# The last merged down step of each superblock: order of weight tile and token half, PSUM banks, and the columns of the last superblock

## The chip, the cores and the metric

The kernel runs on one core of a Trainium2 chip. A core has one matrix engine (TensorE, PE in the profile), three engines for elementwise work (VectorE or DVE, ScalarE or ACT, GpSimd or POOL), a queue engine that issues transfers (SyncE or SP) and 16 DMA engines. Matmul results land in PSUM, which has eight banks; all else lies in SBUF. The metric is the device time of one execution in microseconds. Before the change it is 2521.25 us, the median of 3 runs (2519.53 to 2521.3).

## The reference

One layer of a hybrid decoder runs over 2048 prompt tokens and 64 sample tokens of width 1024, all in fp32. Ahead of the MLP stand an RMS norm, one input projection, window attention and a pooling mixer side by side, an output projection, and cross attention into 256 memory tokens. What bears on the change is the MLP, the last norm, and the first lines of the next tokens:

```python
h = _rmsnorm(x, g_mix)
proj = h @ w_in
...
h = _rmsnorm(x, g_ffn)
x = x + jnp.square(jax.nn.relu(h @ w_up)) @ w_down
...
y_prompt = _rmsnorm(xp, g_final)
y_sample = _rmsnorm(xs, g_final)
```

`w_in` is 1024 x 1280, `w_up` 1024 x 4096 and `w_down` 4096 x 1024; the RMS norm is x * rsqrt(mean(x*x) + 1e-5) * g.

## The kernel before

**Tokens.** The 2112 tokens run in three superblocks of two blocks each, 384 + 384, then 256 + 320 (64 of them sample tokens), then 384 + 384. Activations are kept with the width of 1024 as eight pieces of 128 partitions (k or m from 0 to 7) and the tokens as columns. A superblock goes from the input projection (matmuls on L352 to L354) and attention through cross attention to the MLP, and is followed by the next one; the first superblock begins at once, the last one is followed by nothing.

**Numbers.** Each fp32 factor is split into a high and a low part, and each product takes three matmuls, high by high, high by low, low by high (`mm3`, L109 to L114). A weight tile of 128 x 1024 is fetched into one of six fp32 buffers f, and split by ACT (the high half, L118) and DVE (the low half, L119) into two of twelve buffers w.

**The MLP.** It runs over 16 pairs of 128-wide hidden tiles. For each, `up` makes the squared ReLU of both token halves in seven products, and `down` adds hidden times `w_down` to x. For the last two pairs there is one merged `down` with `fin=True`: 16 groups (8 output pieces m, 2 token halves h), each with 4 hidden tiles by 3 matmuls = 12 matmuls into one PSUM bank, after which DVE adds the bank to x (L1381). The weights come as two tiles, t = 0 for m from 0 to 3 and t = 1 for m from 4 to 7, each as four w buffers for two pairs. In the merged step the order is h outer, t inner: t=0 and t=1 for the first half, then both again for the second. All 16 groups take their bank from the four banks MM; the other four banks, AUX, serve norms and attention. In the second superblock the first half has the 256 columns of block 0 and 32 of block 1, the second half the other 288 of block 1; in the other two superblocks a half is a block.

**The last norm.** After each group of the merged step `Norm.sq` squares the finished piece on ACT and adds it to a running sum on DVE (L250). After the eighth piece of a block `final` takes the sum over partitions by one matmul with a matrix of ones (L258; in the last superblock's second block it is eight such matmuls, one for each piece, on L242), inverts the root with a logarithm, an exponential and three rows on DVE (L261 to L265), scales the eight pieces of x (L1402, eight rows) and sends them out in four transfers (L1404).

**What sets the order.** Weights are requested ahead in a fixed order by `Stream.pump`, up to five, as long as enough w and f buffers stay free. The next superblock's first weights (`in_win`) can therefore be requested only when the merged step gives back the w buffers of a tile. At that time the first block's x for the next superblock is fetched, normalised and split in pieces (`norm1_sums`, L300 to L302), the second block's from the hook at the fifth half-tile step on; each holds four of the six f buffers meanwhile. `flush` runs such deferred work a piece at a time, and `final` is deferred work as well (`DEFF` = 2 and 2: two flushes later). A scheduler then orders the rows of each engine; each engine executes its own rows in that order.

Of the kernel before, what the change touches and what calls it, by code (L numbers as in the profile page):

```python
# [14 lines left out]
P = 128  # L15
# [36 lines left out]
def kernel(ctx: ExitStack, tc: tile.TileContext, io, nW=12, nF=6, nT=10):  # L52
# [175 lines left out]
    class Norm:  # L228
        def __init__(self, n, x, on_pe=False, add=None):
            self.n, self.x, self.on_pe, self.add = n, x, on_pe, add or nc.vector  # L230
            self.acc = None
            self.pm = AUX.get() if on_pe else None

        def sq(self, k, eng=None):
            n = self.n
            if self.on_pe:
                t = TS.get()
                if eng is None:
                    nc.scalar.activation(t[:, 0:n], self.x(k), AF.Square)
                else:  # L240
                    eng.tensor_tensor(t[:, 0:n], self.x(k), self.x(k), ALU.mult)
                nc.tensor.matmul(self.pm[:, 0:n], ones[:], t[:, 0:n], start=k == 0, stop=k == 7)  # L242
# [4 lines left out]
            else:  # L247
# [3 lines left out]
                TS.put(t)  # L251

# [324 lines left out]
    def superblock(s, blks, nxt):  # L577
# [725 lines left out]
        def relu2(H, h, k, t):  # L1303
# [3 lines left out]
            hi, lo = H[4 * h + 2 * k], H[4 * h + 2 * k + 1]  # L1307
# [54 lines left out]
        def down(pl, Hs, fin=False, hook=None):  # L1362
            K = range(2 * len(pl))
            seq = [(t, h) for h in (0, 1) for t in (0, 1)] if fin else [(t, h) for t in (0, 1) for h in (1, 0)]
            loaded, left, steps = {}, {}, 0
            if fin:
                for bl in blks:
                    bl.norm = Norm(bl.n, bl.x, on_pe=last and bl.b == 1)
            for t, h in seq:
# [3 lines left out]
                w = loaded[t]  # L1373
                for m4 in range(4):
                    m = 4 * t + m4
                    ps = MM.get()
                    mm3(ps[:, 0:hn], K, lambda k: w8(w[k // 2][0])[:, 2 * m4 + k % 2, :], lambda k: w8(w[k // 2][1])[:, 2 * m4 + k % 2, :],
                        lambda k: Hs[k // 2][4 * h + 2 * (k % 2)], lambda k: Hs[k // 2][4 * h + 2 * (k % 2) + 1])
                    for bl, c0, o, n in halves[h]:
                        x = bl.x(m, c0, c0 + n)  # L1380
                        nc.vector.tensor_tensor(x, ps[:, o:o + n], x, ALU.add)  # L1381
                    if fin:
                        blks[h].norm.sq(m)
                    MM.put(ps)
                    if m4 == 3 or fin and m4 == 1:
# [9 lines left out]
                if fin and t == 1:  # L1395
                    later.append([DEFF[h], lambda h=h: final(blks[h])])

        def final(bl):
            bl.norm.fin()
            n = bl.n  # L1400
# [184 lines left out]
```

## Time and profile before

| what | value |
|---|---|
| time, median of 3 runs | 2521.25 us (2519.53 to 2521.3) |
| the profiled execution | 2526.65 us |
| its span in the trace | 2524.6 us |
| its mean granted clock of PE | 0.992 |
| busy: PE, DVE, ACT, POOL | 98%, 74%, 44%, 7% of the span |
| first matmul of the second superblock's input projection | 959.3 us |
| first matmul of the third one's | 1662.95 us |
| first matmul of the last merged step | 2472.86 us |

Times in the profile are microseconds from the span's start. A row of a timeline has start, length, engine, line, operation, output<-inputs and shape; `xN` at its end means N rows run together, and brackets give the idle time of the engine before it and what ended it. A row of a group has line, engine, operation, shapes and count, then the busy time, the mean ns of one, and the idle time ahead of it. Matmuls overlap their neighbours, so the distance between starts, not the length, is what one costs.

### The profile page before, as it was taken

The numbers are of one execution on the slowest core, as the hardware profiler recorded it, in microseconds if no ns is written. First come the engines' busy times: TensorE is split into PE (matmuls) and PEld (weight loads), VectorE is DVE, ScalarE is ACT, GpSimd is POOL, SyncE is SP. The second block draws the span as 40 slices with busy tenths as digits, with TensorE's granted clock in tenths as the row PEclk, the third lists the DMA queues.
The fourth block names the chain that finished last, engine by engine and source line by source line (L and its number), as shares of the span: only waits on it lengthen the run. The fifth ranks groups of instructions, "written<-read, shape, count | busy, mean of one in ns | idle before, by whom it ended". The sixth has DMA issues, their size and how long they took to land.

```text
span 2524.6 us, 38966 instructions
## 1 busy us (share of the span) xinstructions
PE 2479.4 (98%) x15199; PEld 2368.9 (94%) x15199; DVE 1860.2 (74%) x3687; ACT 1099.5 (44%) x2131; POOL 172.8 (7%) x282
## 2 busy tenths in 40 slices
PE   9999999999999999999999999989999999999998
PEld 8798989999999999896799999989998999999997
DVE  8668537877877787764698877888745877777775
ACT  7666335433333344653554434447534533333332
POOL 0015010000000001401000000003301000000000
PEclk9999999999999999899999999999999999999999
DMA  8833211122221125146633232240412122221211
GB/s 290 271 122 105 84 42 59 63 80 69 86 71 62 65 92 164 49 168 214 237 105 109 86 111 93 88 144 26 143 42 76 34 69 67 68 68 67 67 58 50
DMA packets 94844, 250.24 MB, mean 99 GB/s; under 512 B 17028, under 2 KB 31812, under 8 KB 93508
## 3 DMA queue, kind: packets, MB, share of 16 engines
q1 hardware_dynamic: 94660, 247.76, 29.5%
q8 instruction: 119, 1.95, 0.3%
q14 instruction: 65, 0.53, 0.1%
HBM read 225.03 MB, written 22.69 MB: 98 GB/s over the span
## 4 chain that ended last, share of the span: by engine, by line
PE 54%; DVE 3%; ACT 1%; DMA 1%; POOL 1%; issue 0%; POOLq 0%; DVEq 0%; ACTq 0%; SPq 0%
PE mm L112 8%; PE mm L113 8%; PE mm L114 7%; PE aux L114 5%; PE aux L113 5%; PE aux L112 5%; PE mm L354 4%; PE mm L353 4%; PE mm L352 4%; PE aux L772 1%; PE aux L803 1%; PE aux L1105 0%; DVE x L1402 0%; DVE w L119 0%; PE aux L1018 0%
## 5 line engine op out<-in xcount | busy, mean ns | idle before, releaser
L118 ACT CAST w<-f 128x1024 fp32r<-128x1024 f32 x378 | 395.7, 1050 | 723.3 <-PE mm L114 354.2
L119 DVE TENSOR_TENSOR w<-f,w 128x1024 fp32r<-128x1024 f32 x378 | 460.8, 1223 | 178.8 <-PE aux L113 93.3
L113 PE MATMUL mm<-act,w 128*128 128x384 f32 (+2 forms) x1812 | 578.6, 320 | 0.0
L114 PE MATMUL mm<-act,w 128*128 128x384 f32 (+2 forms) x1812 | 576.6, 319 | 1.9 <-DVE w L119 1.9
L112 PE MATMUL mm<-act,w 128*128 128x384 f32 (+2 forms) x1812 | 563.5, 321 | 3.6 <-ACT t L246 2.3
L352 PE MATMUL mm<-act,w 128*128 128x384 f32 (+2 forms) x1248 | 408.2, 327 | 5.6 <-DVE x L1381 4.0
L354 PE MATMUL mm<-act,w 128*128 128x384 f32 (+2 forms) x1248 | 404.5, 324 | 3.3 <-DVE w L119 3.1
L114 PE MATMUL aux<-act,w 128*128 128x384 f32 (+1 forms) x1260 | 404.1, 321 | 1.5 <-DVE w L119 1.5
L112 PE MATMUL aux<-act,w 128*128 128x384 f32 (+1 forms) x1260 | 405.2, 322 | 0.0
L113 PE MATMUL aux<-act,w 128*128 128x384 f32 (+1 forms) x1260 | 404.7, 321 | 0.0
L353 PE MATMUL mm<-act,w 128*128 128x384 f32 (+2 forms) x1248 | 404.3, 324 | 0.1
L1381 DVE TENSOR_TENSOR x<-mm,x 128x384 f32<-128x384 f32 (+3 forms) x672 | 314.3, 495 | 108.7 <-PE mm L114 104.5
L112 PEld LDWEIGHTS mm<-act,w 128*128 128x128 f32 x1812 | 337.6, 188 | 13.8 <-ACT act L1308 7.5
L113 PEld LDWEIGHTS mm<-act,w 128*128 128x128 f32 x1812 | 341.3, 188 | 5.1 <-DVE act L1309 3.7
L114 PEld LDWEIGHTS mm<-act,w 128*128 128x128 f32 x1812 | 340.9, 188 | 3.3 <-DVE w L119 2.3
L352 PEld LDWEIGHTS mm<-act,w 128*128 128x128 f32 x1248 | 238.1, 191 | 9.9 <-ACT w L118 2.7
L353 PEld LDWEIGHTS mm<-act,w 128*128 128x128 f32 x1248 | 238.1, 191 | 4.9 <-issue 2.3
L354 PEld LDWEIGHTS mm<-act,w 128*128 128x128 f32 x1248 | 238.1, 191 | 4.9 <-DVE w L119 4.5
L114 PEld LDWEIGHTS aux<-act,w 128*128 128x128 f32 x1260 | 237.0, 188 | 1.9 <-DVE w L119 1.8
L113 PEld LDWEIGHTS aux<-act,w 128*128 128x128 f32 x1260 | 237.0, 188 | 0.4
L112 PEld LDWEIGHTS aux<-act,w 128*128 128x128 f32 x1260 | 236.4, 188 | 0.4
L1323 DVE TENSOR_TENSOR t<-aux,t 128x384 f32<-128x384 f32 (+1 forms) x315 | 159.2, 519 | 21.6 <-PE aux L114 15.8
(229 smaller groups left out, 3022.0 us busy)
## 6 DMA issues: line engine op xcount, KB each, us to landing
f<-in_wup SPq DMA_DIRECT2D x96, 512.0 KB, 3.5
f<-in_wdn SPq DMA_DIRECT2D x96, 512.0 KB, 3.7
f<-in_win SPq DMA_DIRECT2D x30, 512.0 KB, 3.7
f<-a_s SPq DMA_DIRECT2D x24, 512.0 KB, 3.6
f<-b_s SPq DMA_DIRECT2D x24, 512.0 KB, 4.5
x<-in_x SPq DMA_DIRECT2D x6, 1536.0 KB, 7.4
f<-in_wco SPq DMA_DIRECT2D x16, 512.0 KB, 5.2
f<-in_cmk SPq DMA_DIRECT2D x16, 512.0 KB, 4.4
```

Source lines behind the costliest of these rows:

```text
L112: nc.tensor.matmul(ps, Wh(k), Hh(k), start=first and i == 0, stop=False)
L113: nc.tensor.matmul(ps, Wh(k), Hl(k), start=False, stop=False)
L114: nc.tensor.matmul(ps, Wl(k), Hh(k), start=False, stop=final and i == last)
L118: nc.scalar.copy(th[:], r[:, 0:1024])
L119: nc.vector.tensor_tensor(tl[:], r[:, 0:1024], f32(th[:]), ALU.subtract)
L352: nc.tensor.matmul(ps[:, 0:n], w8(th)[:, k, :], hi(b, k), start=k == 0, stop=False)
L353: nc.tensor.matmul(ps[:, 0:n], w8(th)[:, k, :], lo(b, k), start=False, stop=False)
L354: newest[0] = nc.tensor.matmul(ps[:, 0:n], w8(tl)[:, k, :], hi(b, k), start=False, stop=k == 7)
L772: nc.tensor.matmul(o, q[:, j, c0:c0 + P], kz[kv][hl][:, so + k0:so + 256], start=hl == 0, stop=hl == 1)
L803: nc.tensor.transpose(ps[:, P * j:P * j + P], u.Lv[:, j, P * kb:P * kb + P], ident[:])
L1323: nc.vector.tensor_tensor(t[:, 0:hn], ps[:, 0:hn], r[:, 0:hn], ALU.add)
L1381: nc.vector.tensor_tensor(x, ps[:, o:o + n], x, ALU.add)
```

## The change

It has four parts. In the first two superblocks the merged step runs the weight tile outside and the token half inside: t=0 for both halves, then t=1 for both. So the four w buffers of t=0 come free at half of the step, and a half's pieces are complete at three quarters (the first) and at the end (the second), where they were complete at a half and at the end. In all superblocks every second group takes its bank from AUX, so eight banks are in use. In the last superblock the halves still stand outside, but the columns are 512 (block 0 and 128 of block 1) and 256, where they were 384 and 384; the hidden tiles lie so that both halves are neighbours, and the deferred work advances after each group. There the last norm runs in three parts of 384, 128 and 256 columns, the last of them with seven squares added on DVE and two matmuls with ones in place of eight. The scaling is spread over flushes also in the last superblock, and y is written in strided transfers.

PE at the end of the second superblock's merged step, before. mm are the MM banks, aux the AUX banks, act the activations, w the weights; L114 is the merged step's last matmul, L352 to L354 are the next superblock's input projection. The ones matmul of block 0 stands 48 rows further ahead:

```order
L114 MATMUL mm0_109<-act13_76,w3_82 128x288
L352 MATMUL mm2_111<-act1_64,w1_80 128x384
L353 MATMUL mm2_111<-act4_67,w1_80 128x384
L352 MATMUL mm3_112<-act1_64,w8_87 128x384
L353 MATMUL mm3_112<-act4_67,w8_87 128x384
L352 MATMUL mm1_110<-act1_64,w0_79 128x384
L353 MATMUL mm1_110<-act4_67,w0_79 128x384
L352 MATMUL mm0_109<-act14_77,w1_80 128x384
L353 MATMUL mm0_109<-act6_69,w1_80 128x384
L354 MATMUL mm2_111<-act1_64,w9_88 128x384
```

The same place now (the lines 352 to 354 are 353 to 355 there):

```order
L114 MATMUL aux0_113<-act13_76,w3_82 128x288
L259 MATMUL aux1_114<-t0_97,ones_125 128x256
L353 MATMUL mm2_111<-act1_64,w1_80 128x384
L354 MATMUL mm2_111<-act4_67,w1_80 128x384
L355 MATMUL mm2_111<-act1_64,w9_88 128x384
```

The ones matmul of block 0 (L259) now stands directly behind the step and ahead of the projection, and the first projection group has its low half (L355) at once, not after four groups' high halves.

SP's requests in the same step, before: `in_x` is the second block's x, `in_win` the first weights of the next superblock.

```order
L543 DMA f2_93<-in_x 128x768
L543 DMA f4_95<-in_x 128x768
L543 DMA f1_92<-in_x 128x768
L543 DMA f3_94<-in_x 128x768
L137 DMA f0_91<-in_win 128x1024
L137 DMA f5_96<-in_win 128x1024
L137 DMA f2_93<-in_win 128x1024
L137 DMA f4_95<-in_win 128x1024
L1404 DMA out_y<-x0_107 128x512 x3
```

And now:

```order
L544 DMA f4_95<-in_x 128x768
L544 DMA f0_91<-in_x 128x768
L137 DMA f3_94<-in_win 128x1024
L137 DMA f5_96<-in_win 128x1024
L544 DMA f2_93<-in_x 128x768
L544 DMA f1_92<-in_x 128x768
L137 DMA f3_94<-in_win 128x1024
L137 DMA f5_96<-in_win 128x1024
L137 DMA f1_92<-in_win 128x1024
L137 DMA f4_95<-in_win 128x1024
L137 DMA f0_91<-in_win 128x1024
L1431 DMA out_y<-x0_107 128x512
```

Two weight requests moved ahead of the second half of the x requests, and the transfers of y from among the weights to behind them.

DVE at the end of the program, before: x is the block, t the norm's vectors, vec the gains.

```order
L1381 TENSOR_TENSOR x1_108<-mm0_109,x1_108 128x384
L263 SCALAR_TENSOR_TENSOR t8_105<-t5_102 128x384
L264 SCALAR_TENSOR_TENSOR t8_105<-aux3_116,t8_105 128x384
L265 SCALAR_TENSOR_TENSOR t5_102<-t8_105,t5_102 128x384
L1402 SCALAR_TENSOR_TENSOR x0_107<-x0_107,vec_129,t5_102 128x384 x8
L1381 TENSOR_TENSOR x1_108<-mm2_111,x1_108 128x384
L1381 TENSOR_TENSOR x1_108<-mm3_112,x1_108 128x384
L1381 TENSOR_TENSOR x1_108<-mm1_110,x1_108 128x384
L263 SCALAR_TENSOR_TENSOR t1_98<-t3_100 128x384
L264 SCALAR_TENSOR_TENSOR t1_98<-aux1_114,t1_98 128x384
L265 SCALAR_TENSOR_TENSOR t3_100<-t1_98,t3_100 128x384
L1402 SCALAR_TENSOR_TENSOR x1_108<-x1_108,vec_129,t3_100 128x384 x8
```

And now (L1406 is the addition to x, L1429 the scaling, L247 the sum of squares):

```order
L1406 TENSOR_TENSOR x1_108<-mm3_112,x1_108 128x256
L1429 SCALAR_TENSOR_TENSOR x1_108<-x1_108,vec_129,t2_99 128x128 x2
L247 TENSOR_TENSOR t8_105<-t8_105,t0_97 128x256
L1406 TENSOR_TENSOR x1_108<-aux1_114,x1_108 128x256
L1406 TENSOR_TENSOR x1_108<-mm1_110,x1_108 128x256
L1406 TENSOR_TENSOR x1_108<-aux2_115,x1_108 128x256
L247 TENSOR_TENSOR t8_105<-t8_105,t5_102 128x256
L247 TENSOR_TENSOR t8_105<-t8_105,t7_104 128x256
L264 SCALAR_TENSOR_TENSOR t3_100<-t6_103 128x256
L265 SCALAR_TENSOR_TENSOR t3_100<-aux3_116,t3_100 128x256
L266 SCALAR_TENSOR_TENSOR t6_103<-t3_100,t6_103 128x256
L1429 SCALAR_TENSOR_TENSOR x1_108<-x1_108,vec_129,t6_103 128x256 x8
```

The first part's scaling is no longer in one piece ahead of the last three additions, the last part has 256 columns instead of 384, and sums of squares are added on DVE.

The diff, cut to what matters:

```diff
@@ -229,17 +229,14 @@
         def __init__(self, n, x, on_pe=False, add=None):
             self.n, self.x, self.on_pe, self.add = n, x, on_pe, add or nc.vector
             self.acc = None
-            self.pm = AUX.get() if on_pe else None
-
-        def sq(self, k, eng=None):
+            self.pm = None
+
+        def sq(self, k):
             n = self.n
-            if self.on_pe:
+            if self.on_pe and k == 7:
                 t = TS.get()
-                if eng is None:
-                    nc.scalar.activation(t[:, 0:n], self.x(k), AF.Square)
-                else:
-                    eng.tensor_tensor(t[:, 0:n], self.x(k), self.x(k), ALU.mult)
-                nc.tensor.matmul(self.pm[:, 0:n], ones[:], t[:, 0:n], start=k == 0, stop=k == 7)
+                nc.scalar.activation(t[:, 0:n], self.x(k), AF.Square)
+                nc.tensor.matmul(self.pm[:, 0:n], ones[:], t[:, 0:n], start=False, stop=True)
                 TS.put(t)
             elif self.acc is None:
                 self.acc = TS.get()
@@ -249,6 +246,10 @@
                 nc.scalar.activation(t[:, 0:n], self.x(k), AF.Square)
                 self.add.tensor_tensor(self.acc[:, 0:n], self.acc[:, 0:n], t[:, 0:n], ALU.add)
                 TS.put(t)
+                if self.on_pe and k == 6:
+                    self.pm = AUX.get()
+                    nc.tensor.matmul(self.pm[:, 0:n], ones[:], self.acc[:, 0:n], start=True, stop=False)
+                    TS.put(self.acc)
 
         def fin(self):
             n = self.n
@@ -1304,7 +1305,7 @@
             for bl, c0, o, w in halves[h]:
                 nc.vector.scalar_tensor_tensor(t[:, o:o + w], t[:, o:o + w], 0.0, bl.r3[:, c0:c0 + w], ALU.max, ALU.mult)
             nc.scalar.activation(t[:, 0:hn], t[:, 0:hn], AF.Square)
-            hi, lo = H[4 * h + 2 * k], H[4 * h + 2 * k + 1]
+            hi, lo = H[4 * k + h], H[4 * k + 2 + h]
             nc.scalar.copy(hi, t[:, 0:hn])
             nc.vector.tensor_tensor(lo, t[:, 0:hn], f32(hi), ALU.subtract)
             TS.put(t)
@@ -1359,30 +1360,55 @@
             S.pump()
             return H
 
-        def down(pl, Hs, fin=False, hook=None):
+        def part(bl, c0, n):
+            p = FB()
+            p.bl, p.c0, p.n = bl, c0, n
+            p.x = lambda k: bl.x(k, c0, c0 + n)
+            return p
+
+
+        cols = []
+        for h in range(2):
+            cols.append((hn, (lambda h: lambda H, k, hl: H[4 * k + 2 * hl + h])(h), halves[h], [part(blks[h], 0, blks[h].n)]))
+        if last:
+            ends = []
+            b0, b1 = blks
+            for c0, n, pieces, parts in (
+                    (0, 512, [(b0, 0, 0, 384), (b1, 0, 384, 128)], [part(b0, 0, 384), part(b1, 0, 128)]),
+                    (512, 256, [(b1, 128, 0, 256)], [part(b1, 128, 256)])):
+                ends.append((n, (lambda c0, n: lambda W, k, hl: W[2 * k + hl][:, c0:c0 + n])(c0, n), pieces, parts))
+
+        def down(pl, Hs, fin=False, hook=None, cols=cols):
             K = range(2 * len(pl))
-            seq = [(t, h) for h in (0, 1) for t in (0, 1)] if fin else [(t, h) for t in (0, 1) for h in (1, 0)]
+            if fin and last:
+                seq = [(t, h) for h in (0, 1) for t in (0, 1)]
+            else:
+                seq = [(t, h) for t in (0, 1) for h in ((0, 1) if fin else (1, 0))]
             loaded, left, steps = {}, {}, 0
             if fin:
-                for bl in blks:
-                    bl.norm = Norm(bl.n, bl.x, on_pe=last and bl.b == 1)
+                for h in range(2):
+                    for p in cols[h][3]:
+                        p.norm = Norm(p.n, p.x, on_pe=last and h == 1)
             for t, h in seq:
                 if t not in loaded:
                     loaded[t] = [S.next(("dn", s, p, t)) for p in pl]
                     left[t] = 2
                 w = loaded[t]
+                n, mv, pieces, parts = cols[h]
                 for m4 in range(4):
                     m = 4 * t + m4
-                    ps = MM.get()
-                    mm3(ps[:, 0:hn], K, lambda k: w8(w[k // 2][0])[:, 2 * m4 + k % 2, :], lambda k: w8(w[k // 2][1])[:, 2 * m4 + k % 2, :],
-                        lambda k: Hs[k // 2][4 * h + 2 * (k % 2)], lambda k: Hs[k // 2][4 * h + 2 * (k % 2) + 1])
-                    for bl, c0, o, n in halves[h]:
-                        x = bl.x(m, c0, c0 + n)
-                        nc.vector.tensor_tensor(x, ps[:, o:o + n], x, ALU.add)
+                    bank = AUX if fin and m4 % 2 else MM
+                    ps = bank.get()
+                    mm3(ps[:, 0:n], K, lambda k: w8(w[k // 2][0])[:, 2 * m4 + k % 2, :], lambda k: w8(w[k // 2][1])[:, 2 * m4 + k % 2, :],
+                        lambda k: mv(Hs[k // 2], k % 2, 0), lambda k: mv(Hs[k // 2], k % 2, 1))
+                    for bl, c0, o, wd in pieces:
+                        x = bl.x(m, c0, c0 + wd)
+                        nc.vector.tensor_tensor(x, ps[:, o:o + wd], x, ALU.add)
                     if fin:
-                        blks[h].norm.sq(m)
-                    MM.put(ps)
-                    if m4 == 3 or fin and m4 == 1:
+                        for p in parts:
+                            p.norm.sq(m)
+                    bank.put(ps)
+                    if m4 == 3 or fin and (m4 == 1 or last):
                         steps += 1
                         if hook is not None:
                             hook(steps)
@@ -1393,18 +1419,19 @@
                         WS.put(*x)
                 S.pump()
                 if fin and t == 1:
-                    later.append([DEFF[h], lambda h=h: final(blks[h])])
-
-        def final(bl):
-            bl.norm.fin()
-            n = bl.n
+                    for i, p in enumerate(parts):
+                        later.append([(1 if last else DEFF[h]) + i, lambda p=p: final(p)])
+
+        def final(p):
+            p.norm.fin()
+            n, yo, bl = p.n, p.bl.xo + 8 * p.c0, p.bl
             for k in range(8):
-                nc.vector.scalar_tensor_tensor(bl.x(k), bl.x(k), vec[:, V_GFINAL + k:V_GFINAL + k + 1], bl.norm.r[:, 0:n], ALU.mult, ALU.mult)
+                nc.vector.scalar_tensor_tensor(p.x(k), p.x(k), vec[:, V_GFINAL + k:V_GFINAL + k + 1], p.norm.r[:, 0:n], ALU.mult, ALU.mult)
                 if k % 2 == 1:
-                    nc.sync.dma_start(io["y"][:, bl.xo + (k - 1) * n:bl.xo + (k + 1) * n], XT[bl.b][:, (k - 1) * n:(k + 1) * n])
-                    if has and k < 7:
+                    nc.sync.dma_start(io["y"][:, yo + (k - 1) * n:yo + (k + 1) * n].rearrange("p (k n) -> p k n", n=n), bl.xv[:, k - 1:k + 1, p.c0:p.c0 + n])
+                    if s > 0 and k < 7:
                         yield
-            TS.put(bl.norm.r)
+            TS.put(p.norm.r)
 
         S.resF = 0
         pre = roots(nxt or ())
@@ -1430,6 +1457,10 @@
             rest0 = norm1_sums(nxt[0])
         Hl = list(tt.values())
         H2 = up(NP - 1)
+        if last:
+
+            H, H2 = [[t[:, PT * i:PT * i + 2 * PT] for t in ts for i in (0, 2)] for ts in (Ht, [x for x in Hl if id(x) not in {id(y) for y in tt.values()}])]
+            cols = ends
         for bl in blks:
             TS.put(bl.r3)
         ACTS.put(*tt.values())
@@ -1439,7 +1470,7 @@
             S.resW = 4
             later.append([1, rest0])
             hook = lambda i: norm1(nxt[1], 1) if i == 5 else None
-        down([NP - 2, NP - 1], [H, H2], True, hook)
+        down([NP - 2, NP - 1], [H, H2], True, hook, cols)
         ACTS.put(*Ht, *Hl)
 
     TS2 = [sb(f"cp{i}", 512) for i in range(2)]
```

More of the change, by code (lines that the diff above doesn't have):

```diff
@@ L1567 @@
             n = npr + ns
-            yb = o["y"][:, 8 * xo:8 * (xo + n)].reshape(P, 8, n).transpose(2, 1, 0).reshape(n, 1024)
-            xo += n
+            ws = (128, 256) if t0 + npr == SEQ else (n,)
+            yb = []
+            for w in ws:
+                yb.append(o["y"][:, 8 * xo:8 * (xo + w)].reshape(P, 8, w).transpose(2, 1, 0).reshape(w, 1024))
+                xo += w
+            yb = np.concatenate(yb, 0)
             yp.append(yb[:npr])
```

## The prediction

> **What bounds the kernel now.** First the busy shares of the page, then the waits of TensorE (PE) at the end of the second superblock, then a table of stretches there.
>
> ```profile
> PE 2479.4 (98%) x15199; PEld 2368.9 (94%) x15199; DVE 1860.2 (74%) x3687; ACT 1099.5 (44%) x2131; POOL 172.8 (7%) x282
> PE mm L352 <- DVE x L1381: 4.0, 2, 2.4
> PE mm L354 <- DVE w L119: 2.4, 1, 2.4
> 1636.84:1662.95 26.11, 26.11 (x197) 25.82 (x195) 25.81 (x69) 17.65 (x40) 0.00 (x0) 1.00 0.37 108
> 1662.95:1671.82 8.87, 2.54 (x9) 1.36 (x9) 8.47 (x19) 4.52 (x9) 0.40 (x2) 0.81 0.38 135
> 1671.82:1675.70 3.88, 3.88 (x13) 3.88 (x14) 3.88 (x5) 0.00 (x0) 0.00 (x0) 0.56 0.89 287
> 1675.70:1720.00 44.30, 44.26 (x264) 43.15 (x263) 31.19 (x81) 20.27 (x49) 3.13 (x7) 1.00 0.27 96
> 1720.00:1800.00 80.00, 78.37 (x477) 72.92 (x477) 72.56 (x195) 61.89 (x162) 37.72 (x51) 1.00 0.25 86
> ```
>
> PE is busy 98% of the span, so the change can only win where PE stands still or runs cold: 45 us in all. (A windows row has time, length, busy time and count of PE, its weight loads, VectorE (DVE), ScalarE (ACT) and POOL, granted clock, DMA share, GB/s.) One such place is 1662.95 to 1675.70, directly behind the merged step of the second superblock. What those 22 matmuls would take at full speed comes from the start times of equal ones.
>
> ```profile
> 2485.09 0.33 PE L112 MATMUL mm<-act,w 128*128 128x384 f32 x1
> 2485.61 0.33 PE L112 MATMUL mm<-act,w 128*128 128x384 f32 x1
> 1890.23 0.39 PE L112 MATMUL mm<-w,act 128*128 128x512 f32 x1
> 1890.91 0.39 PE L112 MATMUL mm<-w,act 128*128 128x512 f32 x1
> 959.32 0.28 PE L352 MATMUL mm<-act,w 128*128 128x256 f32 x1
> 959.67 0.28 PE L352 MATMUL mm<-act,w 128*128 128x256 f32 x1
> ```
>
> Three matmuls lie between the two starts of a pair: 0.52/3 = 0.173 us for 384 columns, 0.68/3 = 0.227 for 512, 0.35/3 = 0.12 for 256. So 22 x 0.173 = 3.8 us of work took 8.87 + 3.88 = 12.75: **9.0 us are lost**. DVE was busy in 25.81 of the 26.11 us before and 8.47 of the 8.87 in it: PE waits for DVE.
>
> **The boundary after the second superblock.** What DVE does there, grouped by form from 1641.7 to 1672, with the first and last DVE rows and the first weight request:
>
> ```profile
> L300 DVE SCALAR_TENSOR_TENSOR t<-f,vec,t 128x384 f32<-128x384 f32 x13 | 7.6, 611 | 0.0
> L302 DVE TENSOR_TENSOR act<-t,act 128x384 fp32r<-128x384 f32 x14 | 7.5, 551 | 0.4 <-ACT act L301 0.4
> L1381 DVE TENSOR_TENSOR x<-mm,x 128x288 f32<-128x288 f32 x8 | 3.4, 449 | 0.0
> L250 DVE TENSOR_TENSOR t<-t,t 128x320 f32<-128x320 f32 x7 | 3.4, 486 | 0.1
> L1402 DVE SCALAR_TENSOR_TENSOR x<-x,vec,t 128x256 f32<-128x256 f32 x6 | 2.7, 479 | 0.0
> L263 DVE SCALAR_TENSOR_TENSOR t<-t 128x256 f32<-128x256 f32 x1 | 0.4, 419 | 0.0
> L119 DVE TENSOR_TENSOR w<-f,w 128x1024 fp32r<-128x1024 f32 x1 | 1.2, 1221 | 0.0
> 1641.70 1.28 DVE L1381 TENSOR_TENSOR x<-mm,x 128x256 f32<-128x256 f32 x5
> 1670.55 1.22 DVE L119 TENSOR_TENSOR w<-f,w 128x1024 fp32r<-128x1024 f32 x1
> 1649.44 11.98 SPq L137 DMA_DIRECT2D f<-in_win  x4
> 1659.12 0.30 ACT L97 CAST w<-kcar 64x128 fp32r<-64x128 f32 x1
> ```
>
> Before, the first weight split's low half (L119) is DVE's last row, at 1671.77, and PE's first L354 starts just then, at 1671.82. In the new order the weight tile of t=0 is free at half of the step instead of three quarters, so its requests and split stand earlier; and the second half's pieces, the final norm of block 0 and its scaling stand later. PE's first row behind the step is now the ones matmul of block 0 (L259), which waits for the last add of block 0's squares on DVE. I counted which DVE rows stood ahead of L119 and now stand behind that add: 5 of L300, 6 of L302, 4 evictions of 288 columns, 4 adds of 320, the 3 Newton rows (L263 to L265) and 6 of L1402; one more L119 stands ahead of it. Rows that follow each other overlap by about 0.08 us, so each costs its mean less that: 5 x 0.53 + 6 x 0.47 + 4 x 0.37 + 4 x 0.40 + 3 x 0.34 + 6 x 0.40 - 1.14 = 10.8. The 30.07 us from 1641.70 to 1671.77 shrink to 19.2, that is to 1660.97.
>
> To this I add an estimated 2 to 2.6 us, since block 0's last squares run on ACT behind the cast of the carry (L97), which in its turn waits for the matmul group that reads the buffers it overwrites, and now stands ahead of those squares. That row began at 1659.12; its price is bounded by nothing and by the 4.52 us that ACT worked in 1662.95 to 1671.82. So the sum is ready at 1663 to 1663.6; PE comes there at about 1662.4, as one fp32 ones matmul of some 0.5 us no longer stands before it. PE waits about 1.3 us including the releases, then about 0.6 and 0.7 for the third and the later weights, whose L119 come one by one at 1.14. Of 9.0 about 2.6 stay and some of the cooled clock: **6 us gained**, with ends 0 and 9. The two waits for the eviction (4.0 in the waits view) go by the eight banks; alone they would only become waits for L119, since the split comes last.
>
> On SP the four y stores of a block now stand behind the weight requests instead of among them, and the second block's x requests between those; DMA was 0.37 and 0.38 busy there, so I cost the queue at nothing.
>
> What is moved behind this point (some 12 us of DVE) costs nothing where DVE has slack: 44.30 - 31.19 = 13.1 us from 1675.70 to 1720. After 1720 DVE is at 72.56 of 80 us, so what is still owed there would come out of PE; I take 0, with 2 as upper bound (inside the end of 0 gained).
>
> **The boundary after the first superblock.** Same move, but nothing to win:
>
> ```profile
> 956.00:984.00 28.00, 28.00 (x199) 27.54 (x198) 27.46 (x56) 11.38 (x22) 7.08 (x8) 1.00 0.66 207
> 984.00:1000.00 16.00, 16.00 (x127) 15.77 (x126) 8.63 (x30) 3.76 (x10) 0.00 (x0) 1.00 0.41 117
> 956.14 4.32 DVE L1402 SCALAR_TENSOR_TENSOR x<-x,vec,t 128x384 f32<-128x384 f32 x8
> ```
>
> PE never waits there. DVE is full until 984 (27.46 of 28), and the eight L1402 of a block, 4.32 us in one piece here, now stand between the evictions of the in-projection. With eight banks in flight and 16.00 - 8.63 = 7.4 us of slack behind I take 0; a block of 4.32 in front of a bank that PE wants is the upper price, and below nothing there is no gain, as PE has no idle time to give.
>
> **The tail.** In the last superblock the order stays, the columns become 512 + 256, and the norm sums of the second part are added on DVE.
>
> ```profile
> 2506.41 4.32 DVE L1402 SCALAR_TENSOR_TENSOR x<-x,vec,t 128x384 f32<-128x384 f32 x8
> 2510.65 1.48 DVE L1381 TENSOR_TENSOR x<-mm,x 128x384 f32<-128x384 f32 x3
> 2515.22 0.56 DVE L263 SCALAR_TENSOR_TENSOR t<-t 128x384 f32<-128x384 f32 x1 [3.09 <-ACT t L262]
> 2517.00 4.32 DVE L1402 SCALAR_TENSOR_TENSOR x<-x,vec,t 128x384 f32<-128x384 f32 x8
> 2510.72 0.34 PE L114 MATMUL mm<-act,w 128*128 128x384 f32 x1
> 2511.81 2.20 PE L242 MATMUL aux<-t,ones 128*128 128x384 f32 x6 [0.75 <-ACT t L239]
> 2507.59 14.10 SPq L1404 DMA_DIRECT2D out_y<-x  x8
> ```
>
> The columns by themselves give nothing: 0.227 + 0.12 against 2 x 0.173. Before, three evictions stand behind the eight L1402 of block 0 and end at 2512.1; three ones matmuls (2.20, two rows each, so 0.735 for one), logarithm and exponential (1.2, from 2514.01 to 2515.22) and three Newton rows (1.78, to 2517.00) follow, then eight L1402 to 2521.32, and 3.3 us for the last store to 2524.6. After: the step begins at 2472.86 as before; its 192 matmuls take 96 x 0.227 + 96 x 0.12 = 33.3, with about 1.2 for the ones matmuls of the first part PE ends at 2507.4. DVE is the later one in the second part, 2494.9 on: eight evictions and six adds of 256 (14 x 0.34 = 4.8), 16 scalings (8 x 0.53, and 8 x 0.25 for 128 columns, estimated from 0.53 for 384 and 0.40 for 256: 6.2), Newton rows of 384 and 128 (2.5), what is left of the first part (1.5), 15.0 in all, and some 1.2 of waits: the last eviction ends near 2511.1, the last add at 2511.8. Then, scaled down from the rows for 384, two ones matmuls of 256 (0.5 each) to 2512.9, logarithm and exponential 0.9, Newton 1.35, eight scalings at 0.40 to 2518.4, and 3.3 for the store: 2521.7 against 2524.6, 2.9 gained. PE is idle for 4.4 us ahead of the last ones matmuls and may be cold for them, 1 us more. **2 us gained**, with ends 1 and 4.
>
> How long an idle time cools PE is shown once more here, by a small hole and what follows:
>
> ```profile
> 1000.00:1004.00 4.00, 3.60 (x28) 3.00 (x27) 1.22 (x4) 3.79 (x14) 1.21 (x3) 1.00 0.00 0
> 1004.00:1008.00 4.00, 3.00 (x17) 2.43 (x16) 2.78 (x7) 1.75 (x6) 1.46 (x2) 0.77 0.20 49
> 1008.00:1020.00 12.00, 12.00 (x51) 11.04 (x52) 1.95 (x7) 1.37 (x5) 0.00 (x0) 0.50 0.35 120
> 1880.00:1920.00 40.00, 40.00 (x191) 33.11 (x189) 16.93 (x32) 16.52 (x39) 6.57 (x14) 1.00 0.16 54
> ```
>
> 1.4 us of idle in 8 us is followed by 12 us at half clock. So even the short waits that I leave at 1663 may cost some clock, which is why I take 6 and not 6.4.
>
> The Trainium skill ("TensorE: Matmul & The Clock Gate", section "HAM oscillation — how this bites in real kernels") has the rule that only idle gaps above some 3.4 us cost clock. By it the waits left at 1663 would cost nothing beyond themselves (6.4 in place of 6), and the tail's 4.4 us would cool PE; the row of 0.50 speaks against it for the first.
>
> **Rivals.** *The waits go altogether*: ACT's cast isn't late and the low halves come in time; 9 + 3, 2509. For it speaks that 10.8 us of DVE work leave the path; against it that PE's first row is a wait for DVE. *The wait is replaced*: DVE stays full as before, and the moved rows come back between the first splits, so at most 2 at the boundary and 2 in the tail: 2517.3 to 2519. For it speaks that DVE worked 25.81 of 26.11 us before, against it the 13.1 us of slack behind. *Slower*: at the first boundary the L1402 of each block hold back an eviction whose bank PE needs next: 4.3 us of wait, and half clock behind it as in 1671.82 to 1675.70, where 13 x 0.173 = 2.25 took 3.88, 1.6 more; two blocks 11.8. With nothing won at the second boundary and 2 in the tail this gives 2531. It needs the bank to be asked for within the 4.3 us; it is slower as soon as both blocks do that and less than 10 are won elsewhere. *512 columns run cold*: half clock in the 96 matmuls of 512 columns, 96 x 0.227 = 21.8 more, 2535. Against it stand such matmuls at 1.00 in the stretch from 1880 to 1920, PE busy 40.00 of 40.
>
> The Trainium skill (the same page, "A second HAM failure mode: psum-queue depth-cycling") tells of a kernel that cycled PSUM banks at 512 columns and swung between half and full clock; that is this last rival, and the trace of 1880 to 1920 disagrees.
>
> **How the numbers follow.** The profiled execution took 2526.65 us (span 2524.6), 5.4 above the median of 2521.25; I subtract the same 8 from both: 2518.65 for such an execution, **2513.3** for the median. Chances: forecast (2510 to 2516) 0.50, waits gone 0.18, wait replaced 0.25, slower 0.05, cold columns 0.02. 0.2%, about what a measurement of this kernel can tell from no change, is 5 us: faster is below 2516.2 (0.50 + 0.18 = 0.68), same up to 2526.3 (0.25), slower 0.07. The range takes in the second rival down to 2508 and most of the third up to 2518.5; outside are the two slow cases and the edges, some 0.15.
>
> **What would show it.** Right: behind the second merged step PE's waits sum to 2 to 3 us in place of 7.5, the first of them an L259 waiting for a DVE add, and the clock stays above 0.9 by 1675; no PE idle time between 950 and 1000; the last L1429 ends some 2.9 us sooner against the step's first matmul. Wrong: L259 or L355 waits over 4 us, DVE full until 1690, L98 evictions waiting at 960 to 980 behind L1429, a clock below 1 in the 512-column part, or PE, not DVE, late in the tail.

## The result, and the profile after

The changed kernel takes 2509.73 us (median of 5 runs, 2507.94 to 2512.65) against 2521.3 us before (median of 5, 2519.53 to 2525.3): ratio 0.995, 95% interval 0.9938 to 0.9961, so 9.8 to 15.6 us less. Forecast were 2513.3 us and a gain of 8. In later series of the kernel before, the medians were 2524.18 us (35 runs) and 2523.97 (11 runs), so the 11.6 us between the two medians here are rather low than high. The profiled execution took 2509.73 us, its span 2507.9.

The page, PE's waits behind the second merged step (window 1600 to 1720), and stretches of the changed kernel, to be held against those of before:

```profile
PE 2467.2 (98%) x15189; PEld 2354.5 (94%) x15189; DVE 1865.3 (74%) x3719; ACT 1101.3 (44%) x2141; POOL 168.9 (7%) x282
PE mm L355 <- DVE w L119: 0.7, 1, 0.7
PE mm L353 <- DVE w L589: 0.2, 1, 0.2
PE aux L773 <- DVE st L774: 0.2, 1, 0.2
```

```profile
1600.00:1654.87 54.87, 54.87 (x415) 54.75 (x414) 46.72 (x106) 29.00 (x56) 0.00 (x0) 1.00 0.36 112
1654.87:1675.00 20.13, 19.76 (x111) 18.91 (x110) 19.87 (x44) 10.06 (x20) 0.55 (x2) 1.00 0.48 157
1675.00:1720.00 45.00, 44.04 (x268) 41.58 (x268) 38.09 (x111) 28.34 (x77) 6.04 (x13) 1.00 0.23 80
1720.00:1800.00 80.00, 79.20 (x473) 74.27 (x472) 63.09 (x159) 52.03 (x130) 36.74 (x48) 1.00 0.32 106
```

Where 12.75 us held 22 matmuls, the 20.13 us from 1654.87 hold 111 rows of them at a clock of 1.00. Of waits 1.1 us are left, where the view of before has 4.0 + 2.4 = 6.4 (the 7.5 that the prediction and the expectation for the order alone name for them stand in no view). DVE is still full (19.87 of 20.13), but with work that nobody waits for; the moved rows show from 1675 to 1720, where DVE is at 38.09 of 45.00 instead of 31.19 of 44.30, and PE is not hurt.

To see where the rest went, the start of the same matmul was read in both traces; between two rows of the table the difference changes only by what lies between them.

| place | before | after | difference |
|---|---|---|---|
| end of the first superblock's MLP | 904.24 | 903.03 | -1.2 |
| in-projection of the second | 989.46 | 988.14 | -1.3 |
| behind its attention | 1109.60 | 1104.45 | -5.2 |
| start of its MLP | 1289.89 | 1284.73 | -5.2 |
| end of its MLP | 1620.57 | 1612.99 | -7.6 |
| in the third superblock | 1807.74 | 1792.67 | -15.1 |
| ahead of the last merged step | 2470.09 | 2455.01 | -15.1 |
| end of the span | 2524.6 | 2507.9 | -16.7 |

So 7.5 us come from the boundary behind the second superblock and 1.6 from the tail. But 2.4 come from inside the second superblock's MLP, where no order changed, and 3.9 from 989 to 1110, where nothing was forecast. 1.2 lie ahead of the first merged step, where only the place of the hidden slices differs; two executions of the kernel before differ by 2.75 us at the same matmul, so nothing can be read from these 1.2. The profiled execution before was 5.4 us above its median, so these terms (16.7) are more than the medians' 11.6.

### The profile page after: what moved, and what is told of

It is laid out like the page before. It is cut to its first block, busy times and chain, and to the rows that moved or that the text cites. A ratio compares the mean times of both kernels' runs of the same rounds, so it can differ in the third digit from the quotient of the medians.

```text
span 2507.9 us, 38993 instructions
## 1 busy us (share of the span) xinstructions
PE 2467.2 (98%) x15189; PEld 2354.5 (94%) x15189; DVE 1865.3 (74%) x3719; ACT 1101.3 (44%) x2141; POOL 168.9 (7%) x282
## 4 chain that ended last, share of the span: by engine, by line
PE 53%; DVE 4%; ACT 1%; DMA 1%; POOL 1%; issue 1%; POOLq 0%; SPq 0%; DVEq 0%; ACTq 0%
PE mm L112 7%; PE mm L113 7%; PE mm L114 7%; PE aux L114 6%; PE aux L112 6%; PE aux L113 6%; PE mm L355 4%; PE mm L354 4%; PE mm L353 4%; PE aux L773 1%; DVE x L1429 1%; DVE w L119 1%; PE aux L804 1%; DMA f<-in_cmk 0%; POOL t L691 0%
## 5 line engine op out<-in xcount | busy, mean ns | idle before, releaser
L119 DVE TENSOR_TENSOR w<-f,w 128x1024 fp32r<-128x1024 f32 x378 | 461.2, 1224 | 176.8 <-PE aux L113 93.4
L113 PE MATMUL mm<-act,w 128*128 128x384 f32 (+2 forms) x1716 | 546.7, 319 | 0.0
L114 PE MATMUL mm<-act,w 128*128 128x384 f32 (+2 forms) x1716 | 544.7, 318 | 1.8 <-DVE w L119 1.8
L112 PE MATMUL mm<-act,w 128*128 128x384 f32 (+2 forms) x1716 | 533.5, 320 | 4.3 <-DVE t L460 2.2
L114 PE MATMUL aux<-act,w 128*128 128x384 f32 (+2 forms) x1356 | 435.0, 321 | 1.5 <-DVE w L119 1.5
L112 PE MATMUL aux<-act,w 128*128 128x384 f32 (+2 forms) x1356 | 436.0, 322 | 0.0
L113 PE MATMUL aux<-act,w 128*128 128x384 f32 (+2 forms) x1356 | 435.9, 321 | 0.0
L353 PE MATMUL mm<-act,w 128*128 128x384 f32 (+2 forms) x1248 | 406.9, 326 | 2.1 <-ACT act L728 1.8
L355 PE MATMUL mm<-act,w 128*128 128x384 f32 (+2 forms) x1248 | 402.6, 323 | 2.3 <-DVE w L119 2.1
L354 PE MATMUL mm<-act,w 128*128 128x384 f32 (+2 forms) x1248 | 402.3, 322 | 0.9 <-DVE act L729 0.9
L1406 DVE TENSOR_TENSOR x<-mm,x 128x384 f32<-128x384 f32 (+3 forms) x648 | 302.3, 494 | 93.9 <-PE mm L114 90.3
L112 PEld LDWEIGHTS mm<-act,w 128*128 128x128 f32 x1716 | 320.0, 189 | 14.5 <-ACT act L1309 7.6
L113 PEld LDWEIGHTS mm<-act,w 128*128 128x128 f32 x1716 | 323.6, 189 | 5.7 <-DVE act L1310 3.5
L114 PEld LDWEIGHTS mm<-act,w 128*128 128x128 f32 x1716 | 323.7, 189 | 3.1 <-DVE w L119 2.2
L114 PEld LDWEIGHTS aux<-act,w 128*128 128x128 f32 x1356 | 255.0, 188 | 2.6 <-DVE w L119 1.8
L113 PEld LDWEIGHTS aux<-act,w 128*128 128x128 f32 x1356 | 255.1, 188 | 1.1
L112 PEld LDWEIGHTS aux<-act,w 128*128 128x128 f32 x1356 | 254.5, 188 | 0.9
L353 PEld LDWEIGHTS mm<-act,w 128*128 128x128 f32 x1248 | 236.4, 189 | 6.8 <-ACT act L728 2.4
L354 PEld LDWEIGHTS mm<-act,w 128*128 128x128 f32 x1248 | 236.5, 189 | 6.3 <-issue 2.3
L355 PEld LDWEIGHTS mm<-act,w 128*128 128x128 f32 x1248 | 236.3, 189 | 4.1 <-DVE w L119 3.8
```

The costliest lines, as they stand in the source:

```text
L112: nc.tensor.matmul(ps, Wh(k), Hh(k), start=first and i == 0, stop=False)
L113: nc.tensor.matmul(ps, Wh(k), Hl(k), start=False, stop=False)
L114: nc.tensor.matmul(ps, Wl(k), Hh(k), start=False, stop=final and i == last)
L119: nc.vector.tensor_tensor(tl[:], r[:, 0:1024], f32(th[:]), ALU.subtract)
L353: nc.tensor.matmul(ps[:, 0:n], w8(th)[:, k, :], hi(b, k), start=k == 0, stop=False)
L354: nc.tensor.matmul(ps[:, 0:n], w8(th)[:, k, :], lo(b, k), start=False, stop=False)
```

## The experiments

**One part at a time.** Four kernels, each the kernel before with one part of the change. The order alone:

```diff
-            seq = [(t, h) for h in (0, 1) for t in (0, 1)] if fin else [(t, h) for t in (0, 1) for h in (1, 0)]
+            if fin and last:
+                seq = [(t, h) for h in (0, 1) for t in (0, 1)]
+            else:
+                seq = [(t, h) for t in (0, 1) for h in ((0, 1) if fin else (1, 0))]
```

> The kernel before with one part of the change: the weight tile outside, the token half inside, in the merged steps of the first two superblocks. Theory A (PE at 1662.95 waits for the DVE queue, and the order takes 10.8 us of DVE work from ahead of the first split): most of the boundary's gain comes from this alone, 5 to 8 us, and PE's waits there fall from 7.5 to under 3 us. Rival B (PE waits for PSUM banks, as the waits view names L1381 for 4.0 of them): the order alone gives at most 3 us, and PE still waits 4 us for evictions.

Measured: ratio 0.9976 (0.9966 to 0.9986), 6.0 us. PE's waits from 1640 to 1720 of this kernel:

```profile
PE mm L354 <- DVE w L119: 0.9, 1, 0.9
PE mm L112 <- DVE x L1384: 0.7, 2, 0.4
PE mm L352 <- DVE x L1384: 0.5, 1, 0.5
```

2.1 us are left of 6.4; in its trace the same matmuls gain 5.4 us between 1624 and 1807 of before. That is the boundary's part; the 6.0 us of the ratio are of the whole program. Theory A holds, with 1.2 us of eviction waits (L1384 is the addition to x here) left.

The eight banks alone:

```diff
-                    ps = MM.get()
+                    bank = AUX if fin and m4 % 2 else MM
+                    ps = bank.get()
...
-                    MM.put(ps)
+                    bank.put(ps)
```

> The kernel before with eight PSUM banks in the three merged steps and nothing else. Theory A: within 1 us of before; the two waits for L1381 at 1662.95 turn into waits for the weight split L119 with the same sum, 7 to 8 us, since the split stays last on DVE. Rival B: 4 us faster, the waits for L1381 go and nothing takes their place.

Measured: ratio 0.9991 (0.998 to 1.0001). PE's waits from 1600 to 1720:

```profile
PE mm L354 <- DVE w L119: 5.0, 1, 5.0
PE mm L352 <- DVE x L1382: 1.9, 1, 1.9
```

6.9 us of waits in place of 6.4 and as much time lost as before: its matmuls stand 3.1 us ahead at 1624 and 3.0 at 1807. Most of the wait moved by name from the eviction to the split, as A said (5.0 for L119; one eviction, L1382, is still waited for, 1.9): the name of a wait is not its price. The 2.3 us of the ratio aren't resolved from nothing.

The place of the hidden slices alone:

```diff
-            hi, lo = H[4 * h + 2 * k], H[4 * h + 2 * k + 1]
+            hi, lo = H[4 * k + h], H[4 * k + 2 + h]
...
-                        lambda k: Hs[k // 2][4 * h + 2 * (k % 2)], lambda k: Hs[k // 2][4 * h + 2 * (k % 2) + 1])
+                        lambda k: Hs[k // 2][4 * (k % 2) + h], lambda k: Hs[k // 2][4 * (k % 2) + 2 + h])
```

> The kernel before with only the places of the hidden tiles' slices changed as in the change (high and low part two slices apart in one tile, not neighbours). Theory A: the 288-column matmuls of the second superblock's down steps run at 0.132 us instead of 0.1345, 12 of them 0.03 us sooner, 2 to 2.5 us over the superblock, and nothing in the other superblocks with 384 columns. Rival C: that drift of 2.4 us between the two traces belongs to the execution, not to the program: 0 us, pitch 0.1345 as before.

Measured: ratio 0.9991 (0.9982 to 1.0). The first matmuls of two groups of one down step, ten groups apart, before and here:

```profile
1549.16 0.30 PE L112 MATMUL mm<-act,w 128*128 128x288 f32 x1
1565.29 0.30 PE L112 MATMUL mm<-act,w 128*128 128x288 f32 x1
```

```profile
1540.93 0.30 PE L112 MATMUL mm<-act,w 128*128 128x288 f32 x1
1556.78 0.30 PE L112 MATMUL mm<-act,w 128*128 128x288 f32 x1
```

16.13 us against 15.85: 1.613 for one group of 12, and 1.585. From 1324 to 1624 of before the kernel gains 2.1 us, in the 384-column MLPs at most 0.5. So the drift belongs to the program, and A holds.

The last superblock alone (columns, eight banks, norm parts, flush after each group). Against the changed kernel, this takes the order, the banks and the layout back in the first two superblocks:

```diff
-            if fin and last:
+            if fin:
...
-                    bank = AUX if fin and m4 % 2 else MM
+                    bank = AUX if fin and last and m4 % 2 else MM
...
-            hi, lo = H[4 * k + h], H[4 * k + 2 + h]
+            hi, lo = (H[4 * k + h], H[4 * k + 2 + h]) if last else (H[4 * h + 2 * k], H[4 * h + 2 * k + 1])
...
```

> The kernel before with only what the change does in the last superblock: columns 512 and 256, eight banks, three parts of the norm, squares added on DVE, a flush after each group. Theory A: 1.5 to 3 us faster, all of it after the last merged step began; PE waits 4 to 5 us for the last add on DVE ahead of its last ones matmuls. Rival D: what the columns win is lost again to that wait and the cold clock behind it: within 0.5 us of before.

Measured: ratio 0.9996 (0.9986 to 1.0006): the time can't tell A from D. The trace can: this kernel is 3.1 us late ahead of the last merged step and 1.5 at the end, so 1.6 us are gained there, as in the changed kernel, and PE waits 4.49 us there for the last add, as A said. The four ratios give 6.0 + 2.3 + 2.3 + 1.0 = 11.6 us, as much as the whole change. But each is uncertain by some 2.5 us, so this does not rule out a joint effect, and the next run shows one.

**Order and banks together.** The order alone left 1.2 us of eviction waits. Both edits above in one kernel:

> The kernel before with the new order in the first two superblocks and eight banks in all merged steps; layout and last superblock as before. Theory A2 (order frees DVE, and only then the four banks become the later wait): the boundary behind the second superblock gives the whole 7.5 us of the change, 2 more than with the order alone, PE's waits there near 1.1 us and none for an eviction. Rival (the order does it all, the difference between the traces is chance): 5.2 us as with the order alone, and the eviction waits of 1.2 us stay or turn into waits for L119.

Measured: ratio 0.9973 (0.9962 to 0.9984), by time no different from the order alone. Its waits from 1640 to 1720:

```profile
PE mm L354 <- DVE w L119: 1.1, 2, 0.7
PE mm L352 <- DVE w L588: 0.2, 1, 0.2
```

No eviction is waited for, 1.3 us are left, and its matmuls gain 7.0 us between 1603 and 1803 of before (2.3 to 9.3 ahead). For comparison, the three executions whose code up to there is the changed kernel's gain 7.5, 6.8 and 7.0 us at this boundary, and five executions with the old order and four banks stray from before by up to 0.5 us. So the 1.6 us between 5.4 and 7.0 are more than this spread, though each is one execution, and A2 holds in the trace: the banks are worth 1 to 2 us, and only once the order has taken the split out of the way.

**The last wait in the tail.** In the changed kernel DVE is the later engine of the last half. The rows of PE and then of DVE:

```profile
2497.03 1.22 PE L251 MATMUL aux<-t,ones 128*128 128x256 f32 x2 [4.48 <-DVE t L247]
2498.04 1.06 PE L239 MATMUL aux<-t,ones 128*128 128x256 f32 x2
```

```profile
2489.52 0.60 DVE L1429 SCALAR_TENSOR_TENSOR x<-x,vec,t 128x128 f32<-128x128 f32 x2
...
2496.03 0.94 DVE L247 TENSOR_TENSOR t<-t,t 128x256 f32<-128x256 f32 x2
2500.10 0.43 DVE L264 SCALAR_TENSOR_TENSOR t<-t 128x256 f32<-128x256 f32 x1 [3.12 <-ACT t L263]
2501.01 0.42 DVE L266 SCALAR_TENSOR_TENSOR t<-t,t 128x256 f32<-128x256 f32 x1
2501.48 3.25 DVE L1429 SCALAR_TENSOR_TENSOR x<-x,vec,t 128x256 f32<-128x256 f32 x8
```

DVE scales other parts ahead of the last additions and then stands idle for 3.12 us. The scaling of the 128-column part can wait until then:

```diff
-        def final(p):
+        def final(p, hold=0):
             p.norm.fin()
+            for _ in range(hold):
+                yield
...
-                        later.append([(1 if last else DEFF[h]) + i, lambda p=p: final(p)])
+                        later.append([(1 if last else DEFF[h]) + i, lambda p=p, i=i: final(p, 7 if last and i else 0)])
```

> The changed kernel with the eight scalings of the 128-column part held back until the last additions are done, so that DVE makes them in the 3.1 us in which it waits for the last norm. Theory A (DVE is the later engine in the last half): PE's last wait falls from 4.5 to about 2.3 us and the end comes 2.2 us sooner after the last merged step's first matmul, 43.5 in place of 45.7... us with the rest unchanged. Rival (the last store or ACT sets the end): the end stays within 0.5 us.

(The two absolute lengths there are miscounted; from the step's first matmul to the end the changed kernel takes some 50 us. The difference is what counts.) Measured: 2508.79 us, ratio to before 0.9938 (0.9924 to 0.9951). PE, and then DVE:

```profile
2493.68 0.70 PE L251 MATMUL aux<-t,ones 128*128 128x256 f32 x2 [2.38 <-DVE t L247]
2494.21 0.59 PE L239 MATMUL aux<-t,ones 128*128 128x256 f32 x2
```

```profile
2493.54 1.92 DVE L1431 SCALAR_TENSOR_TENSOR x<-x,vec,t 128x128 f32<-128x128 f32 x7
2495.80 0.42 DVE L264 SCALAR_TENSOR_TENSOR t<-t 128x256 f32<-128x256 f32 x1 [0.34 <-ACT t L263]
```

PE's wait falls from 4.48 to 2.38, DVE's from 3.12 to 0.34, and from 16.4 us ahead of before at 2403 it comes to 21.0 at the end (2503.6 against 2524.6): 4.6 in the tail instead of 1.6. 2.1 of these 3.0 us are the shorter wait. Another 0.9 is the clock: the two pairs of ones matmuls start 1.01 apart in the changed kernel (2497.03 to 2498.04), but 0.53 here, so each runs half a microsecond longer there. Against the kernel before this version is faster; against the changed kernel the intervals of the ratios overlap, so the 3 us rest on the trace.

**Which neighbours?** The slices once more, high and low part side by side as before, but each tile with one hidden tile:

```diff
-            hi, lo = H[4 * h + 2 * k], H[4 * h + 2 * k + 1]
+            hi, lo = H[4 * k + 2 * h], H[4 * k + 2 * h + 1]
...
-                        lambda k: Hs[k // 2][4 * h + 2 * (k % 2)], lambda k: Hs[k // 2][4 * h + 2 * (k % 2) + 1])
+                        lambda k: Hs[k // 2][4 * (k % 2) + 2 * h], lambda k: Hs[k // 2][4 * (k % 2) + 2 * h + 1])
```

> The kernel before with another place of the hidden slices: high and low part stay neighbours (1152 bytes apart in the second superblock), but the two tiles of a pair hold one hidden tile each instead of one token half each. Theory C1 (it is the distance of high and low part): the second superblock's down groups stay at 1.613 us for 12 matmuls. Rival C2 (it is which tile is read): 1.58 us as in the change.

The same two rows, ten groups apart:

```profile
1547.54 0.30 PE L112 MATMUL mm<-act,w 128*128 128x288 f32 x1
1563.67 0.30 PE L112 MATMUL mm<-act,w 128*128 128x288 f32 x1
```

16.13 us, as before; over the second superblock's MLP its matmuls shift by 0.1 us against before. That is for C1. It looks unclean, as of the seven down steps ahead of the merged one the first ran at 1.587 here (the median of its groups) and only the other six at 1.613. But the kernel before, with all seven at 1.613, had its first at 1.587 too when it was run once more, and in the other runs with neighbours five to seven were at 1.613; in five executions with the layout of the change none of 35 was. The products of `up` ran at 1.587 in all of them. What about the addresses sets the price, and why a single step can go without it, stays open.

**The clock behind the first boundary.** From 989 to 1110 the change gained 3.9 us without a wait that explains it. The stretches of before, and then of the changed kernel:

```profile
1000.00:1020.00 20.00, 18.59 (x93) 16.47 (x93) 5.94 (x17) 6.92 (x24) 2.67 (x4) 0.65 0.25 82
1020.00:1070.00 50.00, 46.90 (x318) 43.79 (x318) 44.22 (x149) 39.74 (x121) 24.70 (x47) 0.93 0.10 32
```

```profile
950.00:1000.00 50.00, 50.00 (x360) 49.11 (x359) 41.23 (x97) 20.79 (x49) 3.19 (x8) 1.00 0.59 179
1000.00:1020.00 20.00, 18.59 (x107) 16.77 (x106) 8.30 (x30) 6.22 (x20) 2.67 (x4) 0.74 0.30 93
1020.00:1070.00 50.00, 46.92 (x332) 43.59 (x332) 46.73 (x142) 43.16 (x127) 28.17 (x50) 1.00 0.19 63
```

PE's busy time is the same, its clock isn't. The kernel before, unchanged, and then the changed kernel and the one with the layout, once more each, for their clock:

> The kernel before, once more, for its clock. If the 17.1 us at half clock from 1006 belong to the program, they are there again; if they hang on where the clock's steps fall in an execution, they are shorter or elsewhere, as in the runs that share the code up to there (3.4 to 17.1 us).

> The changed kernel once more, for its clock. The kernel before showed 17.1 and 3.4 us at half clock between 1006 and 1068 in both its profiles, the changed kernel 3.4 and 6.8. If that belongs to the program, the changed kernel shows some 10 us again and PE has gained 3 to 4 us there; if it is chance, the figure may lie anywhere between 3 and 21.

> The kernel with only the layout changed once more, for its clock: 6.8 us at half clock from 1010 if it belongs to the program, anywhere between 3 and 21 if it is chance. Its down groups of 288 columns should be at 1.58 to 1.59 us again, with none or few at 1.613.

The trace's clock record has half clock from 1008.9 for 17.1 us and from 1066.9 for 3.4 in the second execution of before, as in the first (from 1006.2 and 1064.2). The changed kernel has 3.4 and 6.8 us again (from 1004.0 and 1010.8; first from 1004.6 and 1011.4), the kernel with the layout 3.4 and 6.8 (first 6.8 alone), and its groups are at 1.58 to 1.59 again. The two kernels with only the last superblock or the neighbours changed have 17.1 and 3.4 like before; those with the order, with the banks, and with both have 3.4, 10.2 and 13.6. So far this looks like a property of the program, and the two traces differ by 3 to 4 us through it.

But the repeats don't settle that. In each of the twelve traces every start of half clock lies on one grid of 3.413 us, and the grid stands elsewhere in each execution. Counted from the same matmul (L879 at 1005.12 in the kernel before), the grid stood 1.05 to 1.08 us later in exactly the four executions with 17.1 and 3.4, and 0.51 to 0.95 later in exactly the four with 3.4 and 6.8; the other four, at 0.06, 1.31, 1.81 and 2.29, had other patterns. Both executions of before had the same place of the grid (1.08 and 1.05), so the repeat could not tell the program from the place. The two executions with the layout alone had different places (2.29 and 0.51) and 6.8 against 10.2 us; the kernel with the held scalings, which up to there is the changed kernel, had 6.8 and 3.4, from 1010.0 and 1057.8. And over the 46 runs of before that came with the experiments the mean granted clock lies between 0.991 and 0.996, which by estimate (twice the missing share of a span of some 2520 us) is 45 to 20 us at half clock in a run. So the half-clock time is not fixed by the program, and that the change gains 3 to 4 us by it in other executions is not shown.

## Why the prediction was right, point by point

- **The boundary behind the second superblock**, forecast 6 (0 to 9), measured 7.5 in the trace shown, 6.8 and 7.0 in two more executions. The mechanism is the one forecast: the moved DVE rows leave the path, the split comes early, and the banks alone would only change the wait's name. The size was off in one term, the allowance of 2 to 2.6 us for ACT. These rows of DVE and PE in the changed kernel show it:

```profile
1654.01 0.42 DVE L247 TENSOR_TENSOR t<-t,t 128x256 f32<-128x256 f32 x1
1654.87 0.59 PE L259 MATMUL aux<-t,ones 128*128 128x256 f32 x2
1655.12 0.52 PE L353 MATMUL mm<-act,w 128*128 128x384 f32 x1
1655.65 0.34 PE L355 MATMUL mm<-act,w 128*128 128x384 f32 x1
```

  The last add ends at 1654.43; with the 7.6 us by which the trace is ahead here that is 1662.0, not 1663 to 1663.6, and 0.4 ahead of PE, which comes at 1662.5 (forecast 1662.4). Some 1.0 us stood where 2 to 2.6 were allowed. So the wait of 1.3 us for the sum did not happen, and of the two weight waits of 0.6 and 0.7 one came, with 0.7; the clock stayed at 1.00. Of the 9.0 us lost before, the idle time was 8.87 - 2.54 = 6.3; some 2.2 more, by estimate half of the 4.49 us that PE worked in it, were the half clock from 1668.4 for 6.8 us, which the changed kernel does not have there. The rival "the wait is replaced" falls with this, and "the waits go altogether" (9) lay 1.5 too far.
- **The boundary behind the first superblock**, forecast 0. PE was busy 50.00 of 50.00 us from 950 to 1000, so the moved scalings cost nothing, and the slower rival falls. What the forecast did not have is the half clock after 1000; these two traces differ by 3 to 4 us in it, for a cause that is not shown.
- **The tail**, forecast 2, measured 1.6. PE's idle time was to be 4.4 us and was 4.48; the cold clock was to cost 1 us and cost 0.9 by the run with the shorter wait. The last add was to come 38.9 us behind the step's first matmul and came after 39.2. Of the prediction's signs two did not come: no L259 waited, and the last scaling ended 1.5 us sooner against the step's first matmul, not 2.9, a figure that leaves out the cold clock which the forecast of 2 has in it. The columns win nothing in themselves, and the matmuls of 512 columns ran at full speed. The step's matmuls took 34.7 us and PE was never idle in them:

```profile
2457.80:2492.50 34.70, 34.70 (x197) 29.89 (x196) 23.10 (x61) 11.41 (x30) 0.00 (x0) 1.00 0.09 32
2492.50:2507.90 15.40, 2.12 (x5) 1.17 (x4) 8.90 (x23) 2.42 (x6) 0.00 (x0) 0.62 0.38 135
```

  That ends the rival of cold 512-column matmuls (the clock is 1.00 in that row), though all eight banks are in turn here. The Trainium skill ("TensorE: Matmul & The Clock Gate", section "A second HAM failure mode: psum-queue depth-cycling") tells of a bf16 kernel with 512 columns and cycled banks in which short idle times between groups made the clock swing; this trace shows neither such idle times nor a swing. The same page's rule on idle gaps ("HAM oscillation — how this bites in real kernels") agrees with the tail: behind 4.48 us of idle the ones matmuls ran at half speed, behind 2.38 they did not (1.01 against 0.53 us). It does not agree with the kernel before at 1668.4, where half clock began behind idle times of 2.43 and 1.52 us.
- **The layout of the hidden slices** was not costed at all, as a part that moves no time: 2.1 to 2.4 us in the trace. It is the omitted term that, with the 1.5 us at the boundary, carries most of the distance from 8 to 11.6; the clock after 1000 is the third, as far as it holds outside a profile.
- **What was luck.** The parts that the prediction costed were to give 6 + 0 + 2 = 8 us and gave 7.5 + 0 + 1.6 = 9.1 in the trace. The gain of 8 itself lies below the measured 9.8 to 15.6. The two terms that the sum did not have, the layout and the clock after 1000, both went towards a gain in these traces; nothing in the prediction said that they would.

## What to carry to other kernels

Where PE waits for a queue on another engine, price the queue and not the wait that the profile names: the banks alone took away most of the named wait and won nothing there, the order shortened the queue and won 5.4 us there. Look then for idle time on the engine that is now late, and move into it work that nobody waits for, as the held scalings were. And count a changed address as a change: where an operand lies was worth 2 us here. A difference of clock between two traces is not yet the change's: compare first where the clock's steps lie in each.

## What was not expected of the hardware

- Twelve 288-column matmuls took 1.613 us with the high and low slices neighbours in the tile (1152 bytes apart), and 1.580 to 1.594 with them two slices apart. In seven executions with neighbours 42 of 49 down steps ran at 1.613 and seven at 1.587, one of these in a second run of the very kernel before. At 384 columns no such difference showed.
- The time at half clock between 1000 and 1070 went from 3.4 to 20.5 us in twelve traces, with PE busy for 18.59 us of 1000 to 1020 both before and in the changed kernel. In each trace the starts lay on a grid of 3.413 us, and the pattern was 17.1 and 3.4 us in all four in which the grid stood 1.05 to 1.08 us behind the same matmul.
- Half clock could begin without idle time: in the changed kernel it began at 1011.4, and PE was busy for 3.40 of the 3.40 us from 1008.0 on, some two thirds of them with matmuls of 32 columns (L898).
